# A hybrid attention layer on one core: late gates ahead of the merges, merged rows and output weights split once, output projection tile by tile

## The chip, the cores and the metric

The kernel runs on one core of one Trainium2 chip. The metric is the device time of one execution in microseconds (us); the time of a version is the median of its runs. PE is TensorE (matmuls; PEld are its weight loads), DVE is VectorE, ACT is ScalarE, POOL is GpSimd and SP is SyncE, which issues nearly all DMAs of this kernel.

## The reference

One layer of an encoder on 1024 tokens of width 1024, batch 1, all in float32. What the change touches is the end of the attention half: two attention branches give `o_a` (512 wide) and `o_b` (256 wide); each is projected to 1024, multiplied by a sigmoid gate, and the sum goes through the output projection.

```python
proj = h @ w_in[l]
qa, ka, va, qb, kb, vb, gates = jnp.split(proj, split_at, axis=-1)
...
gate_a, gate_b = jnp.split(jax.nn.sigmoid(gates + b_gate[l]), 2, axis=-1)
merged = gate_a * (o_a @ w_proj_a[l]) + gate_b * (o_b @ w_proj_b[l])
x = x + gt1 * (merged @ w_o[l])

h2 = rms_norm(x, g_norm2[l]) * (1.0 + sc2) + sh2
a, up = jnp.split(h2 @ w_ffn_in[l], 2, axis=-1)
x = x + gt2 * ((jax.nn.silu(a) * up) @ w_ffn_out[l])
```

## The kernel before

Each float32 product is made of three matmuls on parts of reduced precision: an operand is split into `hi` (a rounded copy, made by ScalarE) and `lo` (what is left, `raw - hi`, made by GpSimd or VectorE), and TensorE adds hi x hi, hi x lo and lo x hi (`PASS`). `wsplit` does this for a weight tile of 128 x 512 (ScalarE at L101, GpSimd or VectorE at L102); `wload` issues the load of such a tile on SyncE (L94). Raw tiles rotate through 6 slots (`raw`), split ones through 10 pairs (`hi`, `lo`). PSUM has four pairs of banks by the tags t, v, d and s.

The order of TensorE is that of the program text. For the other engines a scheduler chooses the order; each engine, and each DMA queue, then takes its work strictly in that order, so that an instruction that waits holds up all behind it.

The channels of the width lie in 8 rows of 128 (`i` or `k` = 0 to 7), the tokens in two halves (`hf`) of 512 or 8 tiles (`t`) of 128. The stages around the change are these.

- **Gates.** `gates(i, br)` makes row i of branch br's gate: 24 matmuls for each half (L572 through `mm_set`) into bank d or s, and ScalarE's sigmoid from the bank (L821). One call is a block of 48 matmuls. The first eleven halves were made during the attention and lie in DRAM without their sigmoid; `sig_load` fetches them and ScalarE takes the sigmoid (L854).
- **The split of o.** `o_split` fetches the six rows of attention output from DRAM and splits them into `oT` (L853 to L867).
- **Merge.** `merge(i)` does, for each half, 12 matmuls of branch a into bank t and 6 of branch b into bank v (both L572), and VectorE multiplies the two gates by the banks (L838, L839) and adds them (L840). Gate a and the merged row live in `mg`, a tile of 8 x 1024 float32.
- **Combinations.** `w2_combos(k)`, k = 0 to 10, belongs to the FFN after it: it loads four blocks of the FFN's second weight, forms sums and differences of them in place (GpSimd L875 and L877, VectorE L876 and L878) and writes four blocks back to DRAM (L880). It uses four of the six raw slots.
- **Output projection.** `wo_operands(sw, k)` loads and splits the two halves of row k of the output weight, and splits the merged row k for the tiles of the sweep (L963, L964). Three sweeps of tiles 0 to 2, 3 to 5 and 6 to 7 run over all k, six matmuls for a tile and half at L979, so that the weights are loaded and split three times. At the end of a sweep `o_post(t)` forms the new residual stream, its row statistic and the modulated norm of each tile (VectorE L927, L930, L933, L935; `rstd` L113 to L117; GpSimd L936). `o_turn(t)` turns a tile with eight transposes (L945) and splits it into `h2T` (ScalarE L949, VectorE L950). The turns of one sweep lie within the next; the last two lie in the FFN.
- **FFN.** Its first block is 48 matmuls at L572, then `make_t` forms sums of blocks of `h2T` (L994 to L996, and ScalarE and VectorE around L1049), whose first products are L1059.

Before the change the gates, merges and combinations alternate: gates of rows 2 and 3, the split of o, and then for i = 0 to 7 the fetched gates, the gates of row i if i is over 3, merge i, and the combinations that `W2C` gives to i.

Of the kernel before, what the change touches and what calls it, by code (L numbers as in the profile page):

```python
# [15 lines left out]
S = 1024  # L16
# [15 lines left out]
AHEAD, TK = 2, (0, 4, 5)  # L32


@with_exitstack
def hybrid_layer(ctx: ExitStack, tc: tile.TileContext, x, colp, wada1, wada2, bada2, wqkv, wg, wpa, wpb,
# [3 lines left out]
    def pool(name, side, **kw):  # L40
        return tc.alloc_tile_pool(name=name, bufs=1, side=side, reuse_waits="tile", **kw)
# [16 lines left out]
    def bank(tag):  # L58
        return ps.tile([128, 512], F32, tag=tag, name="ps_" + tag)
# [25 lines left out]
    c32 = const.tile([128, 8, 32], F32, name="c32")  # L85
    nc.vector.memset(c32, 0.0)
    nc.vector.tensor_copy(c32[:, :, 0], cact)

    def fview(ap):
        return ap.bitcast(F32)  # L90
# [1 line left out]
    def wload(src, n):  # L92
        raw = wp.tile([128, 512], F32, tag="raw", bufs=NRAW, name="raw")
        nc.sync.dma_start(raw[:, :n], src)  # L94
        return raw[:, :n]
# [29 lines left out]

    ap_ = pool("attn", "right")
    wide = [128, S]

    NBIG = 7

# [96 lines left out]
    rtab = []  # L227

    def rope_tab():
        cs = ap_.tile([128, 8, 32], F32, tag="cs", bufs=1, name="cs")  # L230
# [574 lines left out]
        gate_w(3, br)  # L805
    ap_.release()

    mgp = pool("merged", "right")
    mg = mgp.tile([128, KT, S], F32, name="mg")
    op_ = pool("o", "right")  # L810
    oT = [op_.tile([128, 6, S], F32R, name=f"oT{i}") for i in range(2)]
    def gates(i, br):
        gate_w(i, br)
        for hf in range(2):
            if i * 4 + br * 2 + hf < NPRE:
                continue
            hs = slice(hf * 512, hf * 512 + 512)
# [3 lines left out]
            nc.scalar.activation(sig[i, br][:, hs], pb, AF.Sigmoid, bias=bg_c[:, 8 * br + i:8 * br + i + 1])  # L821

    mw = {}

    def merge_w(i):
        if i < 8 and i not in mw:
            mw[i] = wslot(wpa[i], 512), wslot(wpb[i], 256)

    def merge(i):
        merge_w(i)  # L830
        wa, wb = mw[i]
        for hf in range(2):
            hs = slice(hf * 512, hf * 512 + 512)
            ppa, ppb = bank("t"), bank("v")
            mm_set(ppa, wa, oT, 0, 4, 4, 0, hs)
            mm_set(ppb, wb, oT, 4, 2, 2, 0, hs)
            m, sb = mg[:, i, hs], sig[i, 1][:, hs]
            nc.vector.tensor_mul(m, m, ppa)  # L838
            nc.vector.tensor_mul(sb, sb, ppb)  # L839
            nc.vector.tensor_add(m, m, sb)  # L840

    sig = {}

    def sig_tiles(i):
        sig[i, 0] = mg[:, i, :]
        sig[i, 1] = mg[:, 4 + i, :] if i in (2, 3) else op_.tile(wide, F32, tag="sb", bufs=2, name="sb")

    def sig_load(i):
        for br in range(2):
            for hf in range(2):  # L850
                if i * 4 + br * 2 + hf < NPRE:
                    hs = slice(hf * 512, hf * 512 + 512)
                    nc.sync.dma_start(sig[i, br][:, hs], sig_d[i, br][:, hs])  # L853
                    nc.scalar.activation(sig[i, br][:, hs], sig[i, br][:, hs], AF.Sigmoid)  # L854

    def o_split():
        for pr in (4, 5, 0, 1, 2, 3):
            for hf in range(2):
                hs = slice(hf * 512, hf * 512 + 512)
                raw = wp.tile([128, 512], F32, tag="raw", bufs=NRAW, name="raw")  # L860
                nc.sync.dma_start(raw, o_d[pr][:, hs])
                hi, lo = oT[0][:, pr, hs], oT[1][:, pr, hs]
                if pr < 4:
                    hi, lo = (z[:, pr].rearrange("p (r w) -> p w r", r=16)[:, 32 * hf:32 * hf + 32] for z in oT)
                    raw = raw.rearrange("p (w r) -> p w r", r=16)
                nc.scalar.activation(hi, raw, AF.Copy)
                (nc.gpsimd if hf else nc.vector).tensor_sub(lo, raw, fview(hi))  # L867

    def w2_combos(k):
        b = {}  # L870
        for r in range(2):
            for c in range(2):
                b[r, c] = wload(w2[(k + HT * r) * 128:(k + HT * r + 1) * 128, c * 512:c * 512 + 512], 512)
        t1, t3, t2, t4 = b[0, 0], b[0, 1], b[1, 1], b[1, 0]
        nc.gpsimd.tensor_sub(t1, b[0, 1], b[0, 0])  # L875
        nc.vector.tensor_sub(t3, b[1, 1], b[0, 1])  # L876
        nc.gpsimd.tensor_sub(t2, b[1, 1], t1)  # L877
        nc.vector.tensor_sub(t4, b[1, 0], t2)  # L878
        for n, z in enumerate((t1, t2, t3, t4)):
            nc.sync.dma_start(w2_d[n, k], z)  # L880

    for i in (2, 3):
        sig_tiles(i)
        gates(i, 0)
        gates(i, 1)
        if i == 2:
            o_split()
    for i in (2, 3):
        sig_load(i)
    for i in range(8):  # L890
        if i not in (2, 3):
            sig_tiles(i)
            sig_load(i)
        if i > 3:
            gates(i, 0)
            gates(i, 1)
        merge(i)
        merge_w(i + 1)
        for k in W2C[i]:
            w2_combos(k)  # L900
    op_.release()
    h1l.release()
    h1p.release()

    h2p = pool("h2", "left")
    h2T = [h2p.tile([128, KT, S], F32R, name=f"h2T{i}") for i in range(2)]
    wop = pool("wo", "right")
# [4 lines left out]
    g2row = wop.tile(wide, F32, name="g2row")  # L912
    nc.sync.dma_start(g2row, g2r.to_broadcast([128, 1024]))
    nc.vector.scalar_tensor_tensor(rows["sc2"], rows["sc2"], 1.0, g2row, op0=ALU.add, op1=ALU.mult)

# [33 lines left out]
            nc.scalar.activation(hi, src, AF.Copy)  # L949
            nc.vector.tensor_sub(lo, src, fview(hi))  # L950

    SWEEPS = ((0, 1, 2), (3, 4, 5), (6, 7))
    steps = [(sw, k) for sw in range(3) for k in range(KT)]
    wops = {}

    def wo_operands(sw, k):
        ts = SWEEPS[sw]
        n = len(ts) * 128
        ws = [wsplit(wload(wo[k * 128:(k + 1) * 128, hf * 512:hf * 512 + 512], 512), nc.vector if hf and k % 4 else None)
              for hf in range(2)]  # L960
        mhl = [wp.tile([128, 512], F32R, tag=tg, bufs=NHL, name="m") for tg in ("hi", "lo")]
        src = mg[:, k, ts[0] * 128:ts[0] * 128 + n]
        nc.scalar.activation(mhl[0][:, :n], src, AF.Copy)  # L963
        nc.vector.tensor_sub(mhl[1][:, :n], src, fview(mhl[0][:, :n]))  # L964
        return ws, mhl

    wops = {}
    for s, (sw, k) in enumerate(steps):
        ts = SWEEPS[sw]
# [3 lines left out]
        ws, mhl = wops[sw, k]  # L973
        if k == 0:
            pb = {(t, hf): bank("dsv"[n]) for n, t in enumerate(ts) for hf in range(2)}
        for n, t in enumerate(ts):
            for hf in range(2):
                for i, (a, b) in enumerate(PASS):
                    nc.tensor.matmul(pb[t, hf], mhl[a][:, n * 128:(n + 1) * 128], ws[hf][b],  # L979
                                     start=(k == 0 and i == 0), stop=(k == KT - 1 and i == 2))  # L980
        if sw and TK[sw] <= k < TK[sw] + 3:
            o_turn(ts[0] - 3 + k - TK[sw])
        if k == KT - 1:
            for t in ts:
                o_post(t, [pb[t, 0], pb[t, 1]])

    glate = []
    wj = {}
# [128 lines left out]
    for j, hf in ((0, 0), (HT, 0), (0, 1), (HT, 1)):  # L1117
        ffn1(j, hf)
        if (j, hf) == (HT, 0):
            o_turn(6)  # L1120
            o_turn(7)
            wop.release()
            mgp.release()
# [195 lines left out]
```

## Time and profile before

| what | value |
|---|---|
| runs | 1603.22, 1606.36, 1607.03 us; median 1606.36 |
| the profiled execution | 1605.34 us; span 1603.6 us; mean granted TensorE clock 0.989 |
| TensorE busy | 1542.5 us, 96% of the span |
| VectorE, GpSimd, ScalarE busy | 1026.6, 717.3, 667.1 us |
| late gates to last merge | 635.2 to 823.2 us after the span's start |
| output projection | 823.2 to 933.2 us |
| loads of the output weight | 48 of 256 KB |

The prediction reads four kinds of rows. A row of the windows has the stretch in us, its length, the busy time (and number of instructions) of each engine, the TensorE clock that was granted as a part of full speed, the busy share of the DMA engines and what they moved. A row of the chain of waits has start, length and the instruction on the chain that ended last. A row of a group by source line has shortest, median and longest time in ns, and the first and last start. A row of the timeline has start, length, engine, line and operation, with the idle time before it and what ended it.

### The profile page before, as it was taken

The page shows a single profiled execution, that of the slowest core. Times are in us where ns is not written, and L with a number is a line of the kernel's source. Part 1 is how long each engine was busy: PE and PEld are TensorE (multiplying, and loading weights), DVE is VectorE, ACT ScalarE, POOL GpSimd, SP SyncE. Part 2 cuts the span into 40 slices and gives each one's busy share as a digit, 9 for nine tenths or more (in the row PEclk, how much of TensorE's full clock was granted, in tenths as well). Part 3 has the DMA queues.
Part 4 walks back from the last instruction along what each step waited for, and adds up shares of the span by engine and source line. Part 5 has one row for each costly group of instructions (what it writes and reads, how often), then busy time and mean ns, then how long its engine had stood idle before and what let it go on. Part 6 is the DMA issues. An engine that isn't in the chain of part 4 may idle for free.

```text
span 1603.6 us, 24772 instructions
## 1 busy us (share of the span) xinstructions
PE 1542.5 (96%) x8240; PEld 1289.0 (80%) x8240; DVE 1026.6 (64%) x2188; ACT 667.1 (42%) x1734; POOL 717.3 (45%) x672
## 2 busy tenths in 40 slices
PE   8999999999999999999999886999999999999997
PEld 7888888898888777778887675788888888888886
DVE  6766676766988743342438869866666666435466
ACT  5555555555645443412234533323333333344442
POOL 1432232221101041554425576876666666545566
PEclk9999999999999999999999998999999999999999
DMA  9322231344244351776645531333333333576765
GB/s 342 101 99 80 84 114 46 125 126 128 88 129 134 92 170 61 264 233 208 210 161 175 177 93 40 104 114 105 101 107 101 106 99 119 191 217 197 243 217 177
DMA packets 149056, 227.52 MB, mean 142 GB/s; under 512 B 27312, under 2 KB 65072, under 8 KB 148928
## 3 DMA queue, kind: packets, MB, share of 16 engines
q1 hardware_dynamic: 148928, 225.94, 44.1%
q8 instruction: 65, 1.06, 0.3%
q14 instruction: 63, 0.52, 0.1%
HBM read 172.28 MB, written 53.59 MB: 141 GB/s over the span
## 4 chain that ended last, share of the span: by engine, by line
PE 75%; DVE 12%; DMA 6%; issue 3%; ACT 2%; POOL 2%; SPq 0%; POOLq 0%; DVEq 0%; ACTq 0%
PE ps_d L283 14%; PE ps_t L1059 6%; PE ps_s L1059 6%; PE ps_v L1059 6%; PE ps_d L1059 6%; PE ps_d L594 4%; PE ps_s L572 3%; PE ps_d L572 3%; PE ps_s L1161 3%; PE ps_d L1161 3%; PE ps_v L475 2%; PE ps_s L434 2%; PE ps_v L1161 2%; PE ps_t L1161 2%; PE ps_t L572 2%
## 5 line engine op out<-in xcount | busy, mean ns | idle before, releaser
L102 POOL TENSOR_TENSOR wlo<-raw,whi 128x512 fp32r<-128x512 f32 (+2 forms) x269 | 362.2, 1354 | 466.6 <-ACT whi L101 442.7
L101 ACT ACTIVATE whi<-raw 128x512 fp32r<-128x512 f32 (+2 forms) x418 | 244.1, 604 | 435.3 <-DMA raw<-in_wg_dram 70.9
L283 PE MATMUL ps_d<-whi,hT 128*128 128x384 f32 x1152 | 316.9, 343 | 0.5 <-ACT v L318 0.5
L102 DVE TENSOR_TENSOR wlo<-raw,whi 128x512 fp32r<-128x512 f32 (+1 forms) x149 | 150.9, 1022 | 130.3 <-ACT whi L101 119.9
L283 PEld LDWEIGHTS ps_d<-whi,hT 128*128 128x128 f32 x1152 | 210.3, 188 | 6.2 <-ACT vs L321 3.5
L283 PE MATMUL ps_d<-wlo,hT 128*128 128x384 f32 x576 | 193.7, 336 | 0.9 <-POOL wlo L102 0.9
L283 PEld LDWEIGHTS ps_d<-wlo,hT 128*128 128x128 f32 x576 | 108.5, 188 | 1.5 <-POOL wlo L102 1.5
L313 POOL TENSOR_TENSOR ra<-qn,rtab 128x64 f32<-128x64 f32 x48 | 16.7, 348 | 166.1 <-DVE qn L306 122.3
L996 POOL TENSOR_TENSOR c<-c 128x512 f32<-128x512 f32 x40 | 63.7, 1593 | 50.2 <-DVE c L1109 42.6
L101 ACT ACTIVATE whi<-ws 128x512 fp32r<-128x512 f32 x60 | 37.9, 632 | 115.0 <-DVE ws L1069 30.0
L449 ACT ACTIVATE P<-P,st 128x256 f32<-128x256 f32 (+2 forms) x100 | 46.2, 464 | 69.5 <-DVE st L448 69.4
L1059 PE MATMUL ps_t<-t,whi 128*128 128x512 f32 x160 | 52.3, 408 | 13.3 <-DVE c L995 12.2
L304 DVE TENSOR_REDUCE ss<-sq 128x4 f32<-128x256 f32 x80 | 33.2, 415 | 45.9 <-ACT sq L301 45.8
L449 ACT ACTIVATE P<-P,sx 128x384 f32<-128x384 f32 (+1 forms) x64 | 37.1, 580 | 52.8 <-DVE sx L448 52.8
L475 PE MATMUL ps_v<-PT,v 128*64 128x128 f32 (+1 forms) x672 | 55.0, 284 | 1.6 <-DVE PT L464 1.6
L460 PE MATMUL ps_t<-ident,P 128*128 128x128 f32 (+1 forms) x336 | 51.6, 274 | 4.5 <-DVE P L452 1.9
L995 DVE TENSOR_TENSOR c<-c 128x512 f32<-128x512 f32 x40 | 46.5, 1162 | 14.2 <-ACT c L994 14.2
L594 PE MATMUL ps_d<-hT,whi 128*128 128x512 f32 x176 | 55.4, 396 | 0.0
L434 PE MATMUL ps_s<-qk 64*128 64x256 f32 (+3 forms) x492 | 53.7, 321 | 1.8 <-DVE st L448 1.2
L572 PE MATMUL ps_s<-hT,whi 128*128 128x512 f32 x176 | 54.3, 390 | 0.0
L434 PEld LDWEIGHTS ps_s<-qk 64*128 64x128 f32 (+1 forms) x492 | 34.9, 182 | 23.6 <-issue 12.5
L448 DVE CUSTOM_DVE_ANT_0 P<-ps_s,rb 128x384 f32<-128x384 f32 (+1 forms) x64 | 31.3, 517 | 33.7 <-PE ps_s L434 33.7
(360 smaller groups left out, 4015.8 us busy)
## 6 DMA issues: line engine op xcount, KB each, us to landing
raw<-in_w_dram SPq DMA_DIRECT2D x165, 256.0 KB
ga_d<-c SPq DMA_DIRECT2D x77, 256.0 KB
raw<-ga_d SPq DMA_DIRECT2D x77, 256.0 KB
wa<-in_wada_dram SPq DMA_DIRECT2D x32, 512.0 KB
raw<-in_wqkv_dram SPq DMA_DIRECT2D x80, 192.0 KB
raw<-in_wo_dram SPq DMA_DIRECT2D x48, 256.0 KB
w_d<-raw SPq DMA_DIRECT2D x44, 256.0 KB
raw<-w_d SPq DMA_DIRECT2D x44, 256.0 KB
```

The costliest lines, as they stand in the source:

```text
L101: nc.scalar.activation(hi[:, :n], r, AF.Copy)
L102: (eng or nc.gpsimd).tensor_sub(lo[:, :n], r, fview(hi[:, :n]))
L283: nc.tensor.matmul(pd[:, :384], tok(a, k, t), U.w[k][b][:, :384], start=(k == 0 and i == 0), stop=(k == KT - 1 and i == 2))
L434: nc.tensor.matmul(I.pS[h][:nq, :nk], U.qk[a][hs, I.q0:I.q0 + nq], U.qk[2 + b][hs, I.kb0 * 128:I.kb0 * 128 + nk], start=(i == 0), stop=(i ...
L449: nc.scalar.activation(P[:nq, :nk], P[:nq, :nk], AF.Exp, scale=-1.0, bias=nm, accum_out=sm)
L460: nc.tensor.transpose(pt[:, i * 128:i * 128 + nq], P[:nq, i * 128:(i + 1) * 128], ident[:nq, :nq])
L475: nc.tensor.matmul(po[hs, :nq], U.v[:, I.kb0 + i, hs], I.PT[h][:, i, :nq], start=(i == 0), stop=(i == nkb - 1))
L572: nc.tensor.matmul(pb, wsl[a][:, j * 128:(j + 1) * 128], src[b][:, ksrc + j, hs], start=(done == 0 and j == 0 and i == 0), stop=(done + j ...
L594: nc.tensor.matmul(st["p"], gw[i, br][j][a][:, kk * 128:(kk + 1) * 128], hT[b][:, k, hs], start=(k == 0 and q == 0), stop=(k == 7 and q == 2))
L996: nc.gpsimd.tensor_mul(sg, sg, up) if j not in (0, HT) else nc.vector.tensor_mul(sg, sg, up)
L1059: nc.tensor.matmul(pb, w[p][:, k * 128:(k + 1) * 128], b[q][:, k], start=(k == 0 and i == 0), stop=(k == 3 and i == 2))
L1161: nc.tensor.matmul(pb[m], o[0][a][:, m * 128:(m + 1) * 128], o[1][b], start=(k == 0 and i == 0), stop=(k == HT - 1 and i == 2))
```

## The change

All late gates run first, row by row, with one combination after each block but the first, after which the split of o stands; their sigmoids stay in ten wide slots `sg`. Then the space of the FFN's input `h1` is given free, `h2T` is placed in it, and the eight merges follow in the order 3, 4, 5, 6, 7, 2, 0, 1. A merge's halves use banks t and d, or v and s. After each half ScalarE copies the merged row into `h2T[0]` and VectorE puts the rest into `h2T[1]`; so the merged rows are split once, into the buffer that the turned tiles later overwrite tile by tile. The fetched gates of rows 2, 0 and 1 come back into `sg` slots that merges have freed, and the split output weights of rows 3 to 7 go into more such slots (`wo_keep`), those of rows 2, 0 and 1 into `hi` and `lo` (`wo_slot`). The last two combinations stand after the first merge.

The output projection then goes over the tiles one at a time: 48 matmuls (now L993), the turn of the tile before the last one after the fourth row, and `o_post` after the last row. Of the small parts of the diff, `c32`, `cs` and `g2row` move into slots of other tiles.

```diff
-W2C = ((), (0,), (1, 2), (3,), (4, 5), (6, 7), (8, 9), (10,))
+LATE = (3, 4, 5, 6, 7)
+MORD = (3, 4, 5, 6, 7, 2, 0, 1)
+MSIG = {0: ((2, 0), (2, 1)), 1: ((0, 0), (0, 1)), 2: ((1, 0), (1, 1))}
+MKEEP = {3: 3, 4: 4, 5: 5, 6: 6, 7: 7}
+MSLOT = {5: 2, 6: 0, 7: 1}
+KFIRST, KLAST, OT = (3, 4, 5, 2, 6, 0, 7, 1), (2, 0, 1, 3, 4, 5, 6, 7), 3
...
-            ppa, ppb = bank("t"), bank("v")
+            ppa, ppb = bank("tv"[hf]), bank("ds"[hf])
             mm_set(ppa, wa, oT, 0, 4, 4, 0, hs)
             mm_set(ppb, wb, oT, 4, 2, 2, 0, hs)
-            m, sb = mg[:, i, hs], sig[i, 1][:, hs]
+            m, sb = sig[i, 0, hf], sig[i, 1, hf]
             nc.vector.tensor_mul(m, m, ppa)
             nc.vector.tensor_mul(sb, sb, ppb)
             nc.vector.tensor_add(m, m, sb)
+            nc.scalar.activation(h2T[0][:, i, hs], m, AF.Copy)
+            nc.vector.tensor_sub(h2T[1][:, i, hs], m, fview(h2T[0][:, i, hs]))
...
+    def wo_keep(k):
+        hi, lo = (sgp.tile(wide, F32R, tag="sg", bufs=10, name="wr") for _ in range(2))
+        for hf in range(2):
+            hs = slice(hf * 512, hf * 512 + 512)
+            raw = wo_raw(hf, k)
+            nc.scalar.activation(hi[:, hs], raw, AF.Copy)
+            nc.gpsimd.tensor_sub(lo[:, hs], raw, fview(hi[:, hs]))
+            wow[hf, k] = hi[:, hs], lo[:, hs]
+
+    def wo_slot(k):
+        for hf in range(2):
+            wow[hf, k] = wsplit(wo_raw(hf, k))
+
+    gates(2, 1)
+    n = 0
+    for i in LATE:
+        for br in range(2):
+            gates(i, br)
+            if i == 3 and br == 0:
+                o_split()
+            else:
+                w2_combos(n)
+                n += 1
...
+    for n, i in enumerate(MORD):
+        merge(i)
+        if n == 0:
+            w2_combos(9)
+            w2_combos(10)
+        for z in MSIG.get(n, ()):
+            sig_tile(*z)
+            for hf in range(2):
+                sig_load(*z, hf)
+        if n in MSLOT:
+            wo_slot(MSLOT[n])
+        if n + 1 < 8:
+            merge_w(MORD[n + 1])
+        if n in MKEEP:
+            wo_keep(MKEEP[n])
...
-    for s, (sw, k) in enumerate(steps):
-        ts = SWEEPS[sw]
-        for z in steps[s:s + AHEAD + 1]:
-            if z not in wops:
-                wops[z] = wo_operands(*z)
...
+    for t in range(8):
+        pbs = [bank("dsv"[t % 3]) for _ in range(2)]
+        ko = KFIRST if t == 0 else (KLAST if t == 7 else range(KT))
+        for n, k in enumerate(ko):
+            for hf in range(2):
+                for a, b in PASS:
+                    nc.tensor.matmul(pbs[hf], h2T[a][:, k, t * 128:(t + 1) * 128], wow[hf, k][b],
+                                     start=(n == 0 and (a, b) == PASS[0]), stop=(n == KT - 1 and (a, b) == PASS[2]))
+            if n == OT and t > 1:
+                o_turn(t - 2)
+        o_post(t, pbs)
```

Three places show what the scheduler makes of it. The first is ScalarE at the end of the gates, after the change; `sg_9073` to `sg_9075` are the gates (6, 1), (7, 0) and (7, 1), `whi_10027` and `whi_10033` belong to the weights of the second merge (row 4), `whi_10099` and `whi_10105` to those of the third (row 5).

```order
L836 ACTIVATE sg_9073<-ps_s_9688,cp_78 128x512
L836 ACTIVATE sg_9073<-ps_s_9714,cp_78 128x512
L102 ACTIVATE whi_10027<-raw_10025 128x512
L102 ACTIVATE whi_10033<-raw_10031 128x256
L102 ACTIVATE whi_10099<-raw_10097 128x512
L102 ACTIVATE whi_10105<-raw_10103 128x256
L836 ACTIVATE sg_9074<-ps_d_9768,cp_78 128x512
```

The sigmoid that empties the bank of the first half of gate (7, 0) stands behind the copies of the second and the third merge's weights; before the change a merge's weights stood between the gates of the row before it.

The second is ScalarE in the merges after the change. `L862` is the new copy of a half of a merged row, `L842` the sigmoid of a fetched half, `sg_10017` and `sg_10022` the gates of row 2.

```order
L862 ACTIVATE h2T0_9921<-sg_9066 128x512
L102 ACTIVATE whi_10305<-raw_10303 128x512
L102 ACTIVATE whi_10311<-raw_10309 128x256
L862 ACTIVATE h2T0_9921<-sg_9066 128x512
L842 ACTIVATE sg_10017<-sg_10017 128x512 x2
L842 ACTIVATE sg_10022<-sg_10022 128x512
L862 ACTIVATE h2T0_9921<-sg_9068 128x512
L102 ACTIVATE whi_10377<-raw_10375 128x512
```

Between the copies of merged halves stand copies of later weights and sigmoids of fetched gates; before the change the copies of merged rows (L963) stood in the projection, and the merges put none on ScalarE.

The third is SyncE in the gates after the change: writes of a combination (L889), the loads of the next one (`in_w2_dram`), and the loads of gate weights (`in_wg_dram`).

```order
L889 DMA w2_d_75<-raw_9420 128x512
L889 DMA w2_d_75<-raw_9422 128x512
L889 DMA w2_d_75<-raw_9426 128x512
L95 DMA raw_9500<-in_w2_dram 128x512
L889 DMA w2_d_75<-raw_9424 128x512
L95 DMA raw_9502<-in_w2_dram 128x512
L95 DMA raw_9504<-in_w2_dram 128x512
L95 DMA raw_9506<-in_w2_dram 128x512
L95 DMA raw_9516<-in_wg_dram 128x512
L95 DMA raw_9522<-in_wg_dram 128x512
```

Every gate block has one such round, in which the gate weights stand behind the writes of one combination and the loads of the next; before the change up to two combinations stood after a merge, and none between the two branches of a row.

More of the change, by code (lines that the diff above doesn't have):

```diff
@@ L31 @@
 XE = ("av", "vv", "aa", "aa", "vv", "aa", "va", "va")
-AHEAD, TK = 2, (0, 4, 5)
 @with_exitstack
@@ L84, in hybrid_layer @@
     nc.vector.scalar_tensor_tensor(bg1, bsc1, 1.0, g1_c, op0=ALU.add, op1=ALU.mult)
-    c32 = const.tile([128, 8, 32], F32, name="c32")
-    nc.vector.memset(c32, 0.0)
-    nc.vector.tensor_copy(c32[:, :, 0], cact)
     def fview(ap):
@@ L127, in hybrid_layer @@
     wide = [128, S]
+    c32 = ap_.tile([128, 256], F32, tag="sq", bufs=1, name="c32").rearrange("p (k n) -> p k n", k=8)
+    nc.vector.memset(c32, 0.0)
+    nc.vector.tensor_copy(c32[:, :, 0], cact)
     NBIG = 7
@@ L229, in rope_tab @@
     def rope_tab():
-        cs = ap_.tile([128, 8, 32], F32, tag="cs", bufs=1, name="cs")
+        cs = ap_.tile([128, 4, 64], F32, tag="qn", bufs=5, name="cs").rearrange("p h (a b) -> p (h a) b", b=32)
         nc.sync.dma_start(cs, rope)
@@ L806, in hybrid_layer, with sig_tile @@
     ap_.release()
-    mgp = pool("merged", "right")
-    mg = mgp.tile([128, KT, S], F32, name="mg")
+    sgp = pool("sig", "right")
+    sig = {}
+    def sig_tile(i, br):
+        z = sgp.tile(wide, F32, tag="sg", bufs=10, name="sg")
+        for hf in range(2):
+            sig.setdefault((i, br, hf), z[:, hf * 512:hf * 512 + 512])
+    for i in LATE:
+        for br in range(2):
+            sig_tile(i, br)
+    sig[2, 1, 1] = sgp.tile([128, 512], F32, name="s2")
     op_ = pool("o", "right")
@@ L820, in gates, with sig_load @@
                 mm_set(pb, gw[i, br][j], hT, 4 * j, 4, 8, 4 * j, hs)
-            nc.scalar.activation(sig[i, br][:, hs], pb, AF.Sigmoid, bias=bg_c[:, 8 * br + i:8 * br + i + 1])
+            nc.scalar.activation(sig[i, br, hf], pb, AF.Sigmoid, bias=bg_c[:, 8 * br + i:8 * br + i + 1])
+    def sig_load(i, br, hf):
+        if i * 4 + br * 2 + hf < NPRE:
+            hs = slice(hf * 512, hf * 512 + 512)
+            nc.sync.dma_start(sig[i, br, hf], sig_d[i, br][:, hs])
+            nc.scalar.activation(sig[i, br, hf], sig[i, br, hf], AF.Sigmoid)
     mw = {}
     def merge_w(i):
-        if i < 8 and i not in mw:
+        if i not in mw:
             mw[i] = wslot(wpa[i], 512), wslot(wpb[i], 256)
@@ L840, in merge @@
             nc.vector.tensor_add(m, m, sb)
[L842 to L854, printed above, removed]
+            nc.scalar.activation(h2T[0][:, i, hs], m, AF.Copy)
+            nc.vector.tensor_sub(h2T[1][:, i, hs], m, fview(h2T[0][:, i, hs]))
     def o_split():
@@ L880, in w2_combos, with wo_raw @@
             nc.sync.dma_start(w2_d[n, k], z)
[L882 to L901, printed above, removed]
+    wow = {}
+    def wo_raw(hf, k):
+        return wload(wo[k * 128:(k + 1) * 128, hf * 512:hf * 512 + 512], 512)
+    def wo_keep(k):
+        hi, lo = (sgp.tile(wide, F32R, tag="sg", bufs=10, name="wr") for _ in range(2))
+        for hf in range(2):
+            hs = slice(hf * 512, hf * 512 + 512)
+            raw = wo_raw(hf, k)
[7 more added lines that the diff above has]
+    n = 0
+    for i in LATE:
+        for br in range(2):
+            gates(i, br)
[4 more added lines that the diff above has]
+                n += 1
     h1l.release()
@@ L906, in hybrid_layer @@
     h2T = [h2p.tile([128, KT, S], F32R, name=f"h2T{i}") for i in range(2)]
+    for n, i in enumerate(MORD):
[13 more added lines that the diff above has]
+            wo_keep(MKEEP[n])
+    op_.release()
     wop = pool("wo", "right")
@@ L911, in hybrid_layer @@
         nc.sync.dma_start(rows[nm], mod_d[off:off + 1024].rearrange("(o n) -> o n", o=1).to_broadcast([128, 1024]))
-    g2row = wop.tile(wide, F32, name="g2row")
+    g2row = wop.tile(wide, F32, tag="tm", bufs=4, name="g2row")
     nc.sync.dma_start(g2row, g2r.to_broadcast([128, 1024]))
@@ L1122, in hybrid_layer @@
             wop.release()
-            mgp.release()
+            sgp.release()
             sp = pool("st", "right")
```

27 lines of the change are left out of this document (removed).

## The prediction

> **What bounds the kernel now.** I read the busy shares first, then the chain of waits through the late part, then the windows over it, and last TensorE's waits there.
>
> ```profile
> PE 1542.5 (96%) x8240; PEld 1289.0 (80%) x8240; DVE 1026.6 (64%) x2188; ACT 667.1 (42%) x1734; POOL 717.3 (45%) x672
> ```
>
> TensorE sets the time of the whole program; a change that leaves its matmuls alone can only gain where it stands still or is slow. The chain shows such places, and where TensorE runs back to back it gives the price of each kind of work:
>
> ```profile
> 635.19 3.00 PE ps_s L572 x12
> ...
> 687.98 4.60 PE ps_t L572 x12
> 692.59 1.40 PE ps_v L572 x6
> 693.98 2.81 PE ps_t L572 x12
> ...
> 713.31 10.88 PE ps_s L572 x48
> ...
> 824.62 1.36 PE ps_s L979 x6
> ...
> 893.43 0.87 PE ps_t L945 x8
> ...
> 933.19 10.91 PE ps_v L572 x48
> ```
>
> The change rebuilds what lies between 635.19 (the first late gate) and 933.19 (the first block of the next stage, L572 x48): 298.0 us. The work in it: 504 gate matmuls are 10.5 blocks of 48 at 10.89, 114.4 us; 16 halves of a merge at 2.81 + 1.40, 67.4; 384 projection matmuls, 64 groups of 6 at 1.36, 87.0; six turns at 0.87, 5.2. Together 274.0. **So 24.0 us are lost there, and no reordering of this stretch can gain more.** Where they lie:
>
> ```profile
> core 0: us, PE busy (x) PEld busy (x) DVE busy (x) ACT busy (x) POOL busy (x), PEclk, DMA share, GB/s
> 662.30:823.20 160.90, 157.37 (x675) 127.37 (x674) 61.73 (x73) 31.43 (x54) 66.05 (x52) 0.99 0.60 196
> 823.20:933.20 110.00, 97.34 (x434) 80.05 (x433) 85.21 (x114) 52.69 (x118) 63.95 (x39) 0.95 0.58 196
> 850.00:890.00 40.00, 34.94 (x155) 28.64 (x154) 36.84 (x48) 19.66 (x46) 25.34 (x14) 0.96 0.59 197
> 890.00:933.20 43.20, 35.60 (x162) 29.22 (x161) 36.55 (x53) 23.14 (x53) 27.04 (x17) 0.92 0.51 164
> ```
>
> Gates and merges (to 823.2) lose a few us near 662 to 702; the projection (from 823.2) loses most: 110.0 us elapse, 97.3 busy, part of that at a clock of 0.92 to 0.96. From 850 to 890 VectorE works 36.84 of 40: it splits weights and merged rows while it also finishes tiles, and TensorE waits for it:
>
> ```profile
> PE ps_t L945 <- DVE h2T L950: 8.9, 2, 5.7
> PE ps_d L979 <- DVE m L964: 1.8, 1, 1.8
> ```
>
> **The change, part by part.** *The projection.* 32 of 48 loads of wo go (8.4 MB) with their splits, and 24 copies (L963) and 24 subtractions (L964) of merged rows go to the merges as 16 and 16 larger ones. A tile is now 48 matmuls, 8 x 1.36 = 10.9 us, plus a turn. From 850 to 933 VectorE spent on what goes
>
> ```profile
> L964 DVE TENSOR_TENSOR m<-mg,m 128x256 fp32r<-128x256 f32 (+1 forms) x15 | 16.9, 1128 | 0.0
> L102 DVE TENSOR_TENSOR wlo<-raw,whi 128x512 fp32r<-128x512 f32 x12 | 13.4, 1119 | 5.9 <-ACT whi L101 5.9
> L930 DVE TENSOR_TENSOR xt<-xt,tm 128x512 f32<-128x512 f32 x13 | 11.5, 900 | 0.0
> ```
>
> 16.9 + 13.4 of its 36.84 + 36.55; the other 43.1 finished and turned 6.5 tiles (13 of L930, two a tile): 6.6 us each, which lies beside a tile's 10.9. So I take the projection at its pure 87.0 + 5.2, plus **1 us** of small waits, near the 1.8 of the shortest row above; bounds 0 and 5.7, the longest.
>
> *The combinations.* c0 to c8 now run one to a gate block of 10.9 us, c9 and c10 behind the first merge, all ahead of the merge weights on SyncE. Each is a chain through one set of slots:
>
> ```profile
> 651.40 2.00 DVE oT L867
> ...
> 674.43 0.70 DVE raw L876
> 675.15 3.09 DMA w_d<-raw
> 678.30 4.55 DMA raw<-in_w_dram
> 683.04 0.69 DVE raw L876
> ```
> ```profile
> L875 POOL TENSOR_TENSOR raw<-raw x11: 1277/1286/1297, 661.8 to 784.5; 128x512 f32<-128x512 f32 x11
> L877 POOL TENSOR_TENSOR raw<-raw x11: 1278/1287/1303, 667.1 to 786.6; 128x512 f32<-128x512 f32 x11
> L878 DVE TENSOR_TENSOR raw<-raw x11: 691/1762/1772, 668.5 to 787.9; 128x512 f32<-128x512 f32 x11
> ```
> ```profile
> 732.78 0.69 DVE L876 TENSOR_TENSOR raw<-raw 128x512 f32<-128x512 f32 x1 [12.48 <-DMA raw<-in_w_dram]
> ...
> 742.38 0.69 DVE L876 TENSOR_TENSOR raw<-raw 128x512 f32<-128x512 f32 x1 [5.74 <-DMA raw<-in_w_dram]
> ```
>
> GpSimd's sum 1.29, VectorE's 0.69, the write 3.09, the next load 4.24 to 4.55 and some 0.3 of SyncE's issue: a cycle of 9.7 us. The shortest that the trace has is 674.43 to 683.04, 8.6; the pair at 732.78 and 742.38 is 9.6 apart. If L877 and L878 stand in it too, it is 1.29 + 0.69 + 1.29 + 1.76 + 3.09 + 4.55 = 12.7. I take 9.7, since the pair in the steady part is nearest to it. The first starts where the split of o ends now, about 652 (651.40 + 2.00, less a load of gates that moves behind it). Then c8 is at 652 + 8 x 9.7 = 729.6 and c9 at 739.3. Behind it in the same six slots come the weights of the third merge: L876 to L878 2.0, write 3.1, load 4.3, sum 0.7, write 3.1, load 4.3, issue 0.4, in all 17.8, so 757.1. ScalarE takes its work in program order, and the sigmoid that empties the first merge's second bank stands behind the copies of these weights (first order fence ahead of this text): 757.9 with one copy. TensorE wants that bank after the gates and 12 matmuls, at 635.2 + 114.4 + 2.8 = 752.4. **Stall: 5.5 us**; nothing with a cycle of 8.6, nine times 3.0 = 27 more with 12.7.
>
> *The merges.* All 16 halves now run without gates between them, 4.21 us each on TensorE. VectorE's part of one:
>
> ```profile
> L838 DVE TENSOR_TENSOR mg<-mg,ps_t x16: 673/677/687, 669.6 to 821.9; 128x512 f32<-128x512 f32 x16
> L839 DVE TENSOR_TENSOR sb<-sb,ps_v x12: 673/676/689, 670.2 to 823.3; 128x512 f32<-128x512 f32 x12
> L840 DVE TENSOR_TENSOR mg<-mg,sb x12: 691/1174/1781, 670.9 to 824.0; 128x512 f32<-128x512 f32 x12
> ```
> ```profile
> 742.99 0.68 DVE L838 TENSOR_TENSOR mg<-mg,ps_t 128x512 f32<-128x512 f32 x1
> 743.59 0.68 DVE L839 TENSOR_TENSOR sb<-sb,ps_v 128x512 f32<-128x512 f32 x1
> ...
> 749.19 0.64 ACT L101 ACTIVATE whi<-raw 128x512 fp32r<-128x512 f32 x1 [3.81 <-DMA raw<-in_wg_dram]
> ```
>
> 0.60 to the next start, 0.67, the sum 1.17, then the new copy on ScalarE (0.63, by L101 of the same shape) and the new subtraction, of L840's kind, 1.17: VectorE waits for the copy, so with the handovers 4.3 a half against 4.21. From the end of the first merge on TensorE it needs 3.15 more for that merge (a half less the first piece, which runs before TensorE is done), 12 x 4.3 for the next six, 54.8 together, and 1.4 until the last one's first half gives back the bank that the projection's first tile takes second; 56.2. TensorE wants it at 14 x 4.21 + 0.7 = 59.7. Pure order would hide it. But ScalarE's copies stand behind sigmoids of gates that are fetched back, and a fetch can only be issued once an earlier merge has freed its slot; so do copies of weights. Such a fetch takes
>
> ```profile
> 745.85 0.33 SPq L94 DMA_DIRECT2D raw<-in_wg_dram  x1
> ...
> 776.16 0.38 SPq L94 DMA_DIRECT2D raw<-in_wg_dram  x1
> ...
> 780.91 0.63 ACT L101 ACTIVATE whi<-raw 128x512 fp32r<-128x512 f32 x1 [1.30 <-DMA raw<-in_wg_dram]
> ```
>
> 3.3 us (745.85 to 749.19) to 4.75 (776.16 to 780.91). At 3.6 the walk through ScalarE's order delays six merges by 2.6, 1.9, 0.4, 0.1, 1.5 and 0.9 = 7.4: bank at 63.6, **stall 3.8**; at 4.75 it is 8.7; with all weights early, 0.
>
> *The clock.* After a stall the first half takes 4.60 instead of 2.81 (687.98 above): 1.8 for each of two stalls, with less after the small waits, **3 us**; 0 if both vanish.
>
> *What stays.* The largest single wait of the program,
>
> ```profile
> PE ps_t L1059 <- DVE c L995: 12.2, 1, 12.2
> ```
>
> comes after 933.19 in VectorE's unchanged order behind the last tile, and I leave it at 12.2; if it depends on when VectorE finishes rather than on when TensorE arrives, it shrinks by at most a few us.
>
> **Sum**: -24.0 + 5.5 + 3.8 + 3 + 1 = -10.7. On the profiled execution, 1605.34 with a span of 1603.6, that is 1594.6; this execution lies 1.0 under the median 1606.36, so 1595.7, rounded 1595.5.
>
> **The rivals.** *R1: the stalls vanish* because the cycle is 8.6, as the first pair of the trace has it: c9 at 729.4, weights at 748.0, before 752.4. For it: four loads in flight from one queue. Against: 9.6 in the steady part, and the late copies of the merges, whose weights would have to come early too. Gain 24 less 1 to 4: about 22, so **1584**.
>
> *R2: VectorE becomes the bound of the merges.* The two operations of a half whose inputs all lie in SBUF then take the upper row, 1.77 (L840's 1.781, L878's 1.762), not 1.17: 0.60 + 0.67 + 1.77 + 0.63 + 1.77 = 5.4 a half, 5.3 by pitch. Then the bank is free at 3.9 + 12 x 5.3 + 1.4 = 68.9, up to 76 with the late copies: 9 to 16.6 of stall, 12.5 in the middle, in place of 3.8: -24.0 + 5.5 + 12.5 + 3 + 1 = -2: **1604**, no change that can be told. For it: GpSimd splits weights all through the merges (66.05 of 160.90 us busy in the first window). Against: L838 and L839, with one input in PSUM, never leave 0.67 to 0.69, and L840's median is 1.17.
> The Trainium skill, "SBUF — State Buffer", section "Who interferes with whom", says that a VectorE instruction with two SBUF inputs takes turns with GpSimd for a lock and one with a PSUM input does not; the rows just named agree with it. It speaks against this change, which adds 16 subtractions with two SBUF inputs beside GpSimd's splits: by it the sum would be R2's wherever the two engines overlap throughout.
>
> *R3: slower, by the combinations.* If L877, L878 and the four writes are all in the cycle, it is 12.7, longer than a gate block, and every later weight on SyncE slips: c9 at 652 + 9 x 12.7 = 766.3, the third merge's weights at 784.9, TensorE 32.5 late: -24.0 + 32.5 + 3.8 + 3 + 1 = +16: **1622**. It decides from the cycle at which 9 cycles add the 10.7 of gain: 9.7 + 1.2 = 10.9, a gate block. For it: VectorE waits 51.6 us before L876 for loads in the old order,
>
> ```profile
> DVE raw L876 <- DMA raw<-in_w_dram: 51.6, 8, 12.5
> ```
>
> so the loads come late, not the sums. Against: both pairs above, 8.6 and 9.6, did the same L877, L878 and four writes in less than a gate block.
>
> **How the numbers follow.** Forecast 0.42, R1 0.20, R2 0.15, R3 0.23. 0.3% or 4.8 us is about what a measurement of this kernel can tell from no change. Faster by more: forecast and R1, 0.62; within: R2, 0.15; slower: R3, 0.23. The range: from R1's best, 1606.4 - 23 = 1583, to 1610, which holds R2 and the part of R3 with a cycle just over a gate block; some 0.1 lies above and 0.08 below. The forecast's own range is 1589 to 1601 (gain 5 to 17, from the stalls' bounds).
>
> **What would show it.** In the changed profile: starts of the combinations' first VectorE sum 9.7 apart in the gates; a wait of TensorE at the first merge for ScalarE's sigmoid, about 5.5; halves of a merge 4.3 to 5 apart on VectorE; a wait at the projection's first tile for VectorE, about 4; then groups at 1.36 with no wait over 2 and no clock below 0.96. L861 and L863 at 1.77 instead of 1.17 would show R2; gate blocks that wait for weights would show R3. Wrong altogether it would be if the projection kept waits of 5 us for the turns, or if the stage behind it took the gain back by arriving at the same VectorE work earlier.

## The result and the profile after

No change that can be told: 1606.34 us median of 20 runs (1601.5 to 1613.75) against 1604.99 before (1601.36 to 1611.11); the ratio is 1.0006, 95% interval [0.9995, 1.0018]. The forecast was 10.7 us faster. The profiled execution after took 1608.76 us with a span of 1607.0, so it lies 2.4 above its median; the losses read from it below are those of this one execution.

The windows of the profile after, over the stretches that the change rebuilt (columns as explained above):

```profile
core 0: us, PE busy (x) PEld busy (x) DVE busy (x) ACT busy (x) POOL busy (x), PEclk, DMA share, GB/s
635.20:662.30 27.10, 27.10 (x126) 22.32 (x123) 12.30 (x9) 15.64 (x20) 18.00 (x11) 1.00 0.61 197
662.30:752.00 89.70, 84.46 (x360) 68.85 (x359) 22.09 (x18) 17.06 (x29) 46.09 (x34) 0.96 0.75 253
752.00:823.20 71.20, 67.01 (x277) 53.65 (x276) 37.45 (x49) 27.81 (x51) 28.04 (x23) 0.95 0.48 154
823.20:933.20 110.00, 106.82 (x475) 87.03 (x474) 58.95 (x101) 32.26 (x76) 39.55 (x24) 0.97 0.36 125
```

The projection's window, 97.34 of 110.00 us busy before, is 106.82 now. What it gained, the gates and merges lost: the same 298 us pass until the FFN's first block. The chain of waits of the profile after shows where:

```profile
677.15 3.01 POOL wlo L103 x2
680.15 0.16 SPq L95
680.41 4.66 DMA raw<-in_w_dram
...
727.71 1.27 POOL raw L886
728.99 4.19 DMA w_d<-raw
733.20 3.88 DMA raw<-in_w_dram
...
737.98 1.29 POOL raw L886
739.29 1.77 DVE raw L887
741.09 2.33 DMA w_d<-raw
743.43 4.08 DMA raw<-in_w_dram
...
764.52 0.42 ACT whi L102
764.94 0.59 ACT sg L836
765.57 2.93 PE ps_d L576 x6
768.50 4.16 PE ps_v L576 x12
772.65 1.41 PE ps_s L576 x6
...
833.21 0.63 ACT whi L102
833.84 0.53 ACT h2T L862
834.39 1.34 DVE h2T L863
835.74 0.60 DVE sg L859
836.33 0.61 DVE sg L860
836.99 13.44 PE ps_d L993 x45
850.43 11.10 PE ps_s L993 x48
...
933.41 10.88 PE ps_v L576 x48
```

From 652 to 765 it runs through the combinations and the splits, copies and loads of weights between them, not through TensorE, and it comes to TensorE at 765.57 through the copy of a merge weight and the sigmoid behind it (L102, then L836). TensorE's waits after the change, from 600 to 1010 us:

```profile
PE ps_t L1071 <- DVE c L1007: 12.8, 1, 12.8
PE ps_d L576 <- ACT sg L836: 5.7, 2, 4.2
PE ps_s L576 <- ACT sg L836: 3.7, 1, 3.7
PE ps_d L993 <- DVE sg L860: 3.2, 1, 3.2
```

The losses by stage against the pure work of the prediction are these. The first merge's second bank is taken at 765.57 instead of 752.4: 13.2, of which 9.4 are the waits for sigmoids and about 2.5 the slow clock behind the first long one of them (3.7 us). What is then left of the merges, 67.4 - 2.8 = 64.6, took 67.6, to 833.1: 3.0 more, nearly all in the two rows at 2.93 and 4.16 instead of 1.40 and 2.81. Tile 0 takes 17.3, from 833.1 to 850.43, instead of 10.9: 3.2 of wait and 3.2 of slow clock. Tiles 1 to 7 and six turns take 83.0 instead of 81.4: 1.6. Together 24.2, where the kernel before lost 24.0. Behind the FFN's first block another 2.2 go: from 933.41 to the second product on the summed blocks, the row `ps_v L1071 x12` of the chain at 1009.99, it is 76.6, and 74.4 before (933.19 to 1007.62, at L1059).

### The profile page after: what moved, and what is told of

It reads as the page before. It is cut to its first block, busy times and chain, and to the rows that moved or that the text cites. A ratio compares the mean times of both kernels' runs of the same rounds, so it can differ in the third digit from the quotient of the medians.

```text
span 1607.0 us, 24545 instructions
## 1 busy us (share of the span) xinstructions
PE 1547.5 (96%) x8240; PEld 1292.7 (80%) x8240; DVE 996.6 (62%) x2162; ACT 650.5 (40%) x1694; POOL 694.9 (43%) x658
## 4 chain that ended last, share of the span: by engine, by line
PE 73%; DVE 9%; DMA 8%; POOL 3%; issue 3%; ACT 3%; SPq 0%; POOLq 0%; DVEq 0%; ACTq 0%
PE ps_d L287 13%; PE ps_t L1071 6%; PE ps_s L1071 6%; PE ps_v L1071 6%; PE ps_d L1071 6%; PE ps_d L598 4%; PE ps_d L1173 3%; PE ps_s L1173 3%; DMA raw<-in_w_dram 2%; PE ps_d L993 2%; PE ps_v L1173 2%; PE ps_t L1173 2%; PE ps_v L576 2%; PE ps_s L438 2%; PE ps_v L479 2%
## 5 line engine op out<-in xcount | busy, mean ns | idle before, releaser
L103 POOL TENSOR_TENSOR wlo<-raw,whi 128x512 fp32r<-128x512 f32 (+2 forms) x245 | 327.3, 1343 | 415.4 <-ACT whi L102 411.0
L102 ACT ACTIVATE whi<-raw 128x512 fp32r<-128x512 f32 (+1 forms) x376 | 218.2, 602 | 382.0 <-DMA raw<-in_wg_dram 71.5
L103 DVE TENSOR_TENSOR wlo<-raw,whi 128x512 fp32r<-128x512 f32 (+1 forms) x131 | 130.8, 1008 | 103.8 <-ACT whi L102 94.7
L102 ACT ACTIVATE whi<-ws 128x512 fp32r<-128x512 f32 x60 | 37.9, 632 | 117.0 <-DVE ws L1081 32.1
L1008 POOL TENSOR_TENSOR c<-c 128x512 f32<-128x512 f32 x40 | 63.5, 1588 | 50.2 <-DVE c L1121 42.6
L1071 PE MATMUL ps_t<-t,whi 128*128 128x512 f32 x160 | 52.0, 406 | 14.4 <-DVE c L1007 12.8
L1071 PE MATMUL ps_s<-t,whi 128*128 128x512 f32 x168 | 52.9, 396 | 0.0
```

The costliest lines, as they stand in the source:

```text
L102: nc.scalar.activation(hi[:, :n], r, AF.Copy)
L103: (eng or nc.gpsimd).tensor_sub(lo[:, :n], r, fview(hi[:, :n]))
L1008: nc.gpsimd.tensor_mul(sg, sg, up) if j not in (0, HT) else nc.vector.tensor_mul(sg, sg, up)
L1071: nc.tensor.matmul(pb, w[p][:, k * 128:(k + 1) * 128], b[q][:, k], start=(k == 0 and i == 0), stop=(k == 3 and i == 2))
```

## The experiments

The lines of some of these kernels lie one or two lower or higher than in the changed kernel. The table puts beside the times three moments of the profiled execution of each: when TensorE takes the first merge's second bank, the FFN's first matmul, and that row of twelve matmuls of L1071. The column and the expectations call it L1071 for short; L1071's very first matmul comes earlier, at 980.83 in the changed kernel. The ratio is to the kernel before, run beside each. Its median was 1604.99 beside the change, 1603.02 beside e1 to e4, 1601.44 beside e5 to e7 and 1601.41 beside e8 and e9, so times are compared by the ratios.

| run | ratio, 95% interval | second bank | FFN | L1071 | FFN to L1071 |
|---|---|---|---|---|---|
| before | 1 | | 933.19 | 1007.62 | 74.4 |
| the change | 1.0006 [0.9995, 1.0018] | 765.57 | 933.41 | 1009.99 | 76.6 |
| e1_dve_split | 0.9963 [0.9948, 0.9977] | 758.57 | 922.75 | 999.33 | 76.6 |
| e2_combos_late | 0.9918 [0.9893, 0.9942] | 752.77 | 914.20 | 990.78 | 76.6 |
| e3_tile0_banks | 0.9993 [0.9978, 1.0009] | 761.10 | 923.48 | 1000.10 | 76.6 |
| e4_both | 0.9945 [0.9923, 0.9966] | 754.65 | 917.86 | 997.01 | 79.2 |
| e5_x_slot | 0.9988 [0.9977, 1.0] | 763.14 | 926.18 | 1000.56 | 74.4 |
| e6_late_x | 0.9918 [0.9899, 0.9937] | 750.58 | 912.10 | 986.48 | 74.4 |
| e7_raw8 | 0.9926 [0.9905, 0.9946] | 752.09 | 910.89 | 987.99 | 77.1 |
| e8_raw8_x | 0.9905 [0.9888, 0.9921] | 754.42 | 913.22 | 988.41 | 75.2 |
| e9_before_raw8 | 0.9994 [0.9982, 1.0007] | | 927.08 | 1002.33 | 75.3 |

A moment is that of one execution. In e3 and e5 the compiled programs have the order of the changed kernel on every engine through all gates and merges. Yet their second bank is taken at 761.10 and 763.14 instead of 765.57, TensorE's waits for sigmoids before it are 5.6 and 8.2 us instead of 9.4, and the wait at tile 0, which e5 has in the same place, is 0.4 instead of 3.2. From the first late gate to the FFN it is 290.9 us in e5 and 297.9 in the change. Differences of a few us between two moments are therefore not put down to an edit here.

**The gate weights' split on VectorE.**

```diff
-            gw[i, br] = [wslot(wg[...], 512) for j in range(2)]
+            gw[i, br] = [wsplit(wload(wg[...], 512), nc.vector if i > 3 else None) for j in range(2)]
```

> The rest of each weight of the late gates (rows 4 to 7) is made by VectorE instead of GpSimd; nothing else differs from the changed kernel. Theory A (the combinations' cycle of 10.4 us runs through GpSimd: 3.0 us of gate splits stand between a combination's second sum and the release of the raw slot that the next load takes): the cycle falls to about 9, so the tenth combination starts some 12 us earlier, TensorE's waits for the sigmoids at the end of the gates (9.4 us in the changed kernel) fall under 3, and the time to about 1596. Rival B (DMA throughput sets the cycle: 2.6 MB a block at 253 GB/s is 10.4 us): the cycle stays at 10.2 to 10.5, the waits too, and the time within 3 us of 1606.

The starts of VectorE's first sum of the combinations (L885 in the changed kernel, L886 in this one), the first and the tenth of each; first the changed kernel, then this one:

```profile
653.95 0.69 DVE L885 TENSOR_TENSOR raw<-raw 128x512 f32<-128x512 f32 x1 [3.31 <-DMA raw<-in_w_dram]
...
747.50 0.69 DVE L885 TENSOR_TENSOR raw<-raw 128x512 f32<-128x512 f32 x1 [6.45 <-DMA raw<-in_w_dram]
```
```profile
653.68 0.69 DVE L886 TENSOR_TENSOR raw<-raw 128x512 f32<-128x512 f32 x1 [2.76 <-POOL raw L885]
...
741.62 0.69 DVE L886 TENSOR_TENSOR raw<-raw 128x512 f32<-128x512 f32 x1 [5.64 <-DMA raw<-in_w_dram]
```

Nine cycles take 93.6 us in the changed kernel, 10.4 each (10.2 in e3 and 10.3 in e5), and 87.9 here, 9.8 each. The time falls by about 7 us (1.0006 to 0.9963; 4 to 5 against e3 and e5). TensorE's waits for sigmoids are 5.2 us, where under 3 were expected; that is no clear fall, since e3 has 5.6 with the old splits, and the same holds for the bank, 7.0 earlier than in the change but 2.5 earlier than in e3. So the edit shortens the cycle by 0.4 to 0.6 us, not by 1.4. Rival B, a rate that stays, falls: from 662.3 to 752 the DMA engines moved 267 GB/s here and 253 in the changed kernel.

How much of that is GpSimd's is open. The splits stay in the cycle, now on VectorE, between a gate weight's load and copy and the combination's last difference:

```profile
677.94 5.14 DMA raw<-in_wg_dram
...
683.17 0.64 ACT whi L102
...
683.84 0.06 DVE wlo L103
...
684.82 0.69 DVE raw L888
```

And in the compiled program two of a combination's four loads take slots of gate weights, where it is one in the changed kernel: the edit moved the slots as well.

**The combinations elsewhere.**

```diff
-            else:
+            elif br and i < 7:
                 w2_combos(n)
                 n += 1
...
         o_post(t, pbs)
+        if t < 7:
+            w2_combos(4 + t)
```

with the two behind the first merge taken out.

> Four combinations instead of nine stand in the gates (one behind each second block), and seven in the projection, one behind each of the tiles 0 to 6. Theory (the gate stage lost 13 us to the combinations' traffic and the merges 3 us of slow clock after it): the first merge's second bank is free at 752 to 754 instead of 765.4, and the time falls by about 16 to 1590. Rival (the work only moves: seven combinations with 2.5 us of VectorE and 2 MB each delay the finish and the turns of tiles): new waits of TensorE for turns of 5 us and more in the projection, and the time stays over 1600.

The bank is taken at 752.77, TensorE has no wait in the gates and the merges, and the time is 1590.03, 13 us under the kernel before (ratio 0.9918); 16 were expected. The windows of this run:

```profile
662.30:752.00 89.70, 89.70 (x397) 74.23 (x396) 7.38 (x6) 23.21 (x40) 35.34 (x29) 1.00 0.43 138
752.00:823.20 71.20, 71.20 (x306) 57.27 (x305) 48.19 (x63) 26.45 (x46) 28.70 (x22) 1.00 0.37 127
823.20:933.20 110.00, 108.39 (x493) 88.02 (x492) 71.17 (x112) 29.28 (x74) 55.10 (x34) 1.00 0.70 243
```

TensorE is busy in all of the first two, at full clock, and the window of the projection bears 243 GB/s with VectorE busy for 71 of 110 us: the rival, delayed turns, is not there (TensorE's waits in the projection are 1.4 us in all, in two places, for split output weights).

**The first tile's banks.**

```diff
-        pbs = [bank("dsv"[t % 3]) for _ in range(2)]
+        pbs = [bank(z) for z in ("dt", "sv", "ds", "vd")[t]] if t < 4 else [...]
```

> Only the banks of the projection's tiles differ: tile 0 takes those that the last merge but one has left (d and t), tile 1 s and v, tile 2 d and s, tile 3 v and d. Theory (tile 0 loses 6.4 us: 3.2 waiting for the last merge's bank and about 3 of slow clock behind the wait): the wait of the projection for VectorE's second product (3.2) is gone, tile 0 takes 11 to 12 us instead of 17.3, and the time falls by 5 to 6 to about 1600. Rival (tile 0 would be as late for its last rows or weights): the wait moves to the merged rows' split of the last merge, and the time stays within 2 us of 1606.

> The combinations of the run before and the banks of the third together. If the two losses are separate and add: 1606 - 16 - 6, about 1584, which is the ceiling of 24 us less some 2. If the merges, starting 13 us earlier, only run further ahead of the fetched gates and output weights, more than 4 us of the gain come back as waits in the merges or at tile 0, and the time is 1588 or more.

The first alone is 0.9993, some 2 us under the change and within what can be told from it. The wait for VectorE's second product is gone, but tile 0 now has these waits, for split output weights, and one more of 0.3:

```profile
PE ps_d L993 <- ACT wr L902: 1.1, 1, 1.1
PE ps_d L993 <- POOL wr L903: 1.1, 1, 1.1
```

So 2.5 us of waits stand in place of 3.2. Tile 0 takes 14.5 us, less than the 17.3 of the change but more than the 12.7 of e5 and the 13.5 of e1, which have the old banks: the edit is not shown to gain anything, and of the 10 us by which its FFN begins earlier than that of the change, 7 are there before tile 0. With the late combinations (e4) it is slower than without it (0.9945 against 0.9918, though the intervals overlap): the last tile now leaves a bank v to the FFN's first block, which waits 1.6 us for `o_post` in the middle, and the time from there to L1071 is 79.2. The time, 1594.73, is on the rival's side of 1588; gains that were to add did not.

**The slot of a row vector.**

```diff
-    g2row = wop.tile(wide, F32, tag="tm", bufs=4, name="g2row")
+    g2row = wop.tile(wide, F32, tag="x", bufs=3, name="g2row")
```

> Only the slot of one row vector differs from the changed kernel: g2row takes one of the three x slots instead of one of the four tm slots, which moves the tm slots 12 KB up, away from the FFN's c tiles. Theory (2.2 us are lost in the FFN's start because GpSimd's first sums write to c tiles that lie over the turned tile 7, wait 13.1 us for its transposes and then run beside VectorE's sums, which take 1.73 instead of about 1 us each): GpSimd's four sums run before 953, VectorE's three take 3.0 instead of 5.2, and from the FFN's first matmul to the first of L1071 it is 74.4 as before the change, not 76.6; the time falls by 2. Rival (the 2.2 us come with the later end of the projection's last tile): 76.6 stays.

In the changed kernel the tile of `c` that GpSimd writes first lies, by the addresses of the compiled program, over the `tm` tile that the last turn reads; before the change it lay over `sh2` and `sc2`, which are free earlier. The sums' inputs are tiles 0 to 3, turned long before; what GpSimd waits for is the space. GpSimd's rows of the changed kernel and then of this one:

```profile
958.43 5.98 POOL L1052 TENSOR_TENSOR c<-h2T,h2T 128x512 f32<-128x512 f32 x4 [13.14 <-PE ps_t L980]
```
```profile
938.23 5.03 POOL L1052 TENSOR_TENSOR c<-h2T,h2T 128x512 f32<-128x512 f32 x4
```

and VectorE's three sums that followed the last turn, in the same order:

```profile
961.47 5.19 DVE L1052 TENSOR_TENSOR c<-h2T,h2T 128x512 f32<-128x512 f32 x3
```
```profile
954.24 2.98 DVE L1052 TENSOR_TENSOR c<-h2T,h2T 128x512 f32<-128x512 f32 x3
```

From the FFN to L1071 it is 74.4 again, as the theory has it, and the time is some 3 us under the change (0.9988 to 1.0006, with intervals of 2 us each way). The rival falls by the trace, whatever the time; e6 against e2, 74.4 and 76.6, says the same.

> The late combinations of the second run with that slot. If the two effects add: 1590 - 2, about 1588, some 16 us under the kernel before; with the FFN's start unchanged it is 1590 again.

The stretch is 74.4 here too, but the ratio is 0.9918 as without it: 2 us are not told in intervals of 3 to 4 us each way, and the trace alone shows them.

**More raw slots.**

```diff
-NRAW, NHL = 6, 10
+NRAW, NHL = 8, 9
```

> The changed kernel with 8 raw slots instead of 6 and 9 pairs of split weights instead of 10 (the same space), so that a combination's loads need not wait for the gate weights' slots of the block before. What is read is the gate stage alone, as the other stages change too. Theory A (the cycle is a chain through the slots): starts of the combinations 8.5 to 9.5 us apart instead of 10.4, and the first merge's second bank at 752 to 758. Rival B (throughput of the DMA engines at some 253 to 267 GB/s): 9.8 to 10.4 apart and the bank after 760.

> The 8 raw slots of the run before and the x slot for g2row together. If the two add: from the FFN's first matmul to the first of L1071 some 2 us less than the 77.1 with 8 raw slots alone, and 1588 - 2 = 1586, the fastest of all. If the FFN's start is set by other waits with these slots (a wait of 6.1 for a weight split stands there), it stays at 77 and 1588.

> The kernel before with 8 raw slots and 9 pairs of split weights: a control. Theory (the slots free the gate stage of the changed kernel, whose combinations stand one to a block; the kernel before loses its time in the projection, where VectorE is behind): within 4 us of the kernel before, its projection still 108 to 111 us. Rival (more raw slots help the whole program, and the gain with them has nothing to do with the change): 10 us and more under the kernel before.

With 8 slots, in the rest the changed kernel:

```profile
650.86 1.76 DVE L885 TENSOR_TENSOR raw<-raw 128x512 f32<-128x512 f32 x1 [2.77 <-POOL raw L884]
...
730.27 0.69 DVE L885 TENSOR_TENSOR raw<-raw 128x512 f32<-128x512 f32 x1 [6.60 <-DMA raw<-in_w_dram]
```
```profile
662.30:752.00 89.70, 89.70 (x397) 74.21 (x396) 13.46 (x18) 22.21 (x38) 49.72 (x40) 1.00 0.87 288
823.20:933.20 110.00, 110.00 (x508) 90.49 (x507) 52.91 (x95) 24.29 (x67) 29.24 (x16) 1.00 0.27 101
```

Nine cycles take 79.4 us, 8.8 each; the DMA engines move 288 GB/s in the window where they moved 253; TensorE is busy in the whole of the stretch; and the time is 12 us under the kernel before. In e8 it is 9.0 and 292 GB/s. That settles what bounded the cycle in the gates: the number of raw slots, and not a rate of the DMA engines at 253 to 267 GB/s. The control does nothing of the kind: the kernel before with the same slots is at 0.9994, and its projection takes 108 us, from 818.67 to 927.08, and keeps its waits:

```profile
PE ps_t L945 <- DVE h2T L950: 6.1, 2, 5.1
...
PE ps_d L979 <- DVE m L964: 3.7, 2, 3.2
```

(The shorter of the two waits for `h2T` lies in the FFN.)

So more slots alone gain nothing, and the change alone gains nothing; together they do. With the x slot too, FFN to L1071 is 75.2 instead of 77.1 and the ratio 0.9905, the lowest of all, though its interval overlaps those of e2, e6 and e7. It is about 1% under both kernels. Eight slots together with late combinations were not tried, nor were still more slots, nor the 9 pairs of split weights apart from the 8 slots.

## Why the prediction was wrong

- **The ceiling and the projection**: right. The matmuls run tile by tile without waits for turns; tiles 1 to 7 lost 1.6 us where 1 was allowed. e7, which has no stall before them, keeps TensorE busy in all 110.00 us of that window, and its FFN begins 22 us earlier than that of the change, near the 24.0. Its time gains only 12: some 2.7 go in the FFN (77.1 instead of 74.4), and the rest is that the profiled execution of the kernel before lies 3.9 above this kernel's median beside e7, and e7's own 2.6 under its median.
- **The combinations: the step that failed, by size.** The place and the road were as predicted: third merge's weights, the copy on ScalarE, the sigmoid behind it, the bank. The cycle was put at 9.7 us and is 10.4, so the stall put at 5.5 is 13.2 (10.2 and 10.3, with stalls of 8.7 and 10.7, in e3 and e5). The sum of a cycle was one sum of GpSimd, one of VectorE, a write and a load. The chain has other links. In some cycles it runs through GpSimd's two splits of the gate weights, behind which the next load stands (677.15 to 680.41 above): in the compiled program one of a combination's four loads takes the slot of a gate weight, and SyncE's later loads stand behind it. In the last two cycles ahead of the tenth it runs through GpSimd's second sum (L886), once VectorE's second (L887) too, a write and a load (727.71 to 747.51): terms that the prediction had kept out of its 9.7 and given to R3. How the 0.7 us divides between these links stays open. That e1 comes to 9.8 is no confirmation of the sum, since its chain has yet other links; with two more slots the cycle is 8.8 and the stall is gone (e7). The pairs quoted of the kernel before were two combinations in a row behind one merge, with no gate weights between them. GpSimd's first sum started on time, at 652.1; the tenth began at 745.4 instead of 739.3, which is 6.1 of the 7.7 that were missed, and the last weights came 1.4 later than 17.8 behind it.
- **Merges**: a stall of 3.8 was predicted and 3.2 measured, which is luck: the wait is 1.2 in e1 and 0.4 in e5, and the sizes are others. The subtraction (L863) took 0.69 in the median and 0.87 in the mean, the sum (L861) 0.75 and 1.02, where 1.17 was put for each:

```profile
L863 DVE TENSOR_TENSOR h2T<-sg,h2T x16: 691/694/1366, 770.6 to 843.0; 128x512 fp32r<-128x512 f32 x16
```

  The late copies on ScalarE cost more: VectorE waits 22.6 us in 16 places for L862. Ahead of tile 0's bank such a copy stands behind that of a weight (833.21 above), as the prediction's walk through ScalarE's order had it.
- **The clock**: put at 3, measured 6.2 (3.0 after the gates, 3.2 in tile 0; another 2.5 behind the wait of 3.7 are within the 13.2). The price of one stall, 1.8, was read from one row of 12 matmuls at 4.60, but the slow clock lasts for more of them: 765.57 to 772.65 ran at a granted clock of 0.59.
- **What stays**: wrong by 2.2. The FFN's order was the same, as argued, but the slots under its tiles were not, and a wait for the last turn made GpSimd's sums run beside VectorE's (shown by the traces of e5 and e6).
- **The sum** with the terms of the profiled execution: -24.0 + 13.2 + 3.2 + 6.2 + 1.6 = +0.2 at the FFN, and +2.2 behind it. With 5.5, 3 and 0 for the terms that were off it was -10.7.
- **The rivals**: the time is R2's, about none, but not by R2's mechanism, since L861 and L863 are well under 1.77. It is nearer to R3's, more links in the cycle than the forecast had; R3 was said to decide from a cycle of 10.9, and at 10.4, with the clock and the FFN's start that were too low in the sum, it was enough. e7 has what R1 foresaw, a cycle of 8.8 and no stall, by more slots.

## What to carry to other kernels

Before a prefetch is moved into a busier stage, list for each of its loads whose slot it takes and which engine or write frees that slot: the cycle can run through that engine too, even where it is idle half of the time (GpSimd was busy for 46.09 of 89.70 us in the gates). A change of tags or pool sizes moves other tiles' addresses, and so can put a wait into a stage that the change never names. Two stalls removed do not add up until the one next behind each is known. And before two traces are compared, look at how far two executions of the same program lie apart.

## What the runs showed of the hardware

- TensorE's clock after a wait. Two rows of e3, each the first two matmuls behind a wait (in brackets), and then two of the kernel before:

```profile
707.82 0.74 PE L576 MATMUL ps_d<-hT,whi 128*128 128x512 f32 x2 [2.05 <-ACT sg L836]
...
727.55 1.22 PE L576 MATMUL ps_s<-hT,whi 128*128 128x512 f32 x2 [3.08 <-ACT sg L836]
```
```profile
684.48 0.70 PE L572 MATMUL ps_v<-oT,whi 128*128 128x512 f32 x2 [1.14 <-DVE sb L839]
...
687.98 0.73 PE L572 MATMUL ps_t<-oT,whi 128*128 128x512 f32 x2 [1.87 <-DVE mg L838]
```

  After single waits of 1.55 and 2.05 us TensorE ran on at full rate; after 3.08, 3.45, 3.69 and 4.19 (e3, e1 and the changed kernel) the two took 1.22 and the rate stayed low for 5 to 6 us. The Trainium skill, "TensorE: Matmul & The Clock Gate", section "What's actually happening", puts the drop to half rate behind an idle window of about 3.4 us; here 3.08 was enough and 2.05 was not. Nor does one wait decide alone: in the kernel before, the rate fell just behind the second of two waits of 1.14 and 1.87 us that lie 1.6 us apart, and the granted clock was 0.63 from 687.98 to 692.58.
- VectorE and GpSimd: three sums of two SBUF inputs each took 5.19 us beside GpSimd's and 2.98 with most of GpSimd's work out of the way. In the merges, beside GpSimd's splits, L863 with two SBUF inputs took 0.69 to 1.37 us and L861 0.69 to 1.83, while L859 and L860, with one input in PSUM, had a mean of 0.68. The rule of the Trainium skill, "SBUF — State Buffer", section "Who interferes with whom", which the prediction weighed for the merges, agrees with these rows; in the merges its price was small, and the 2.2 us that TensorE lost by it fell in the FFN.
